# Output projections of a hybrid layer by seven block products instead of eight, with the gMLP phase's buffers kept to the end

## The chip, the cores and the metric

One core of a Trainium2 chip runs the whole layer as one program. The metric is the device time in microseconds, the median of several runs. Engines are called PE (matmul), PEld (its weight load), DVE (vector), ACT (scalar), POOL (GpSimd) and SP (which issues DMAs). Each engine works through its own row of instructions in order and waits where an operand is not there.

## The reference, cut to what matters

```python
proj = rms_norm(x, norm_g) @ w_in                    # 1024 x 1024 by 1024 x N_IN
u, v, z_a, z_b, xbc, dt_raw, g_a, g_b = split(proj)
v = layer_norm(gelu(v)); sv = einsum(tril(w_s), v) + b_s    # per chunk of 128 rows
y_a = gelu(u) * sv * silu(z_a)
y_b = gated_group_rms_norm(ssd_scan(...), z_b)       # 2048 columns
merged = sigmoid(g_a) * (y_a @ w_oa) + sigmoid(g_b) * (y_b @ w_ob)
x = x + merged @ w_out
x = x + sigmoid(rms_norm(x) @ w_pg) * (p @ w_ple)
out = rms_norm(x, final_g)
```

All is in 32-bit floats. The shapes are 1024 rows, width 1024; `w_oa` is 1024x1024, `w_ob` 2048x1024.

## The kernel before, in words

Every large product is made of three: each operand is split into a rounded part `hi` and a residue `lo`, and PE adds hi·hi, hi·lo and lo·hi, 128x512 at a time (L99 to L109). The split of a weight block (L229) is a cast on ACT (L231) and a subtraction on POOL (L232); the results lie in two tags of six buffers.

The phases follow each other: norm and transposes; the SSD branch in four groups; the gMLP phase; the output projections (o phase); `merged @ w_out` (`px`, stage 1); the gate of the last embedding (`ppg`) and the final norm.

The gMLP phase is 17 column pairs (L552): v0 to v3, ga3, then four times gb, za, u. A pair makes a 256 x 1024 piece of a projection, as a 2x2 by 2x2 block product by seven products of 12 matmuls where the plain way has eight. On the weights' side it needs four sums `s1` to `s4` (L561, DVE), seven casts and seven residues; on the side of the normed input the combinations `T1` to `T4` are made once (L527 to L547). Its results come out one by one through an epilogue: the first after the fourth product, the last, `epi(1, 0)`, after the seventh, `T4`. For v it is GELU, four transposes, batch statistics and a copy (L635); for za tanh and two updates on DVE (L682); for u GELU and a product (L691); for gb and ga one tanh (L608). In the program's text a pair's weights stand ahead of its matmuls.

The temporary tiles have tags of their own: epilogue `e` 5, sums `s` 4, `u5` 2, `sv` 4, `bt` 1.

The o phase (L710) has six parts: 512 rows of `y_b` with `w_ob` four times, of `y_a` with `w_oa` twice. A part reads y through POOL's DMA queue (L730), splits it (ACT, and DVE L734), and makes eight blocks `po` of 24 matmuls each; results are added into `m` (L758), in part 3 multiplied by the gate of g_b (L763), in parts 4 and 5 multiplied by that of g_a (L765) and added (L767, L769). After part 0 the pools of the gMLP phase are closed and larger ones opened.

The order on each engine is not the text's: a scheduler that simulates the program (L881) sets it, with the waits for free buffers that pools and tags bring.

Of the kernel before, what the change touches and what calls it, by code (L numbers as in the profile page):

```python
# [29 lines left out]
def kernel(  # L30
# [234 lines left out]
    dth = const.tile([P, NCH, NH], F32, name="dth")  # L265
    dec4 = const.tile([P, NCH, NH], F32, name="dec4")
    cdec = const.tile([P, NCH, NH], F32, name="cdec")
    cs = const.tile([P, NCH, NH], F32, name="cs")
# [280 lines left out]
    for j in range(2, 6):  # L549
        gate_tile(j)  # L550

    def pair(name, col, epi):  # L552

        blk = {}
        for i in range(2):
            raw = wp.tile([P, 4, 2 * P], F32, tag="raw", name=f"raw{i}_{name}")
            nc.sync.dma_start(out=raw, in_=w_in_k[:, 4 * i:4 * i + 4, col:col + 2 * P])
            blk[0, i], blk[1, i] = raw[:, :, 0:P], raw[:, :, P:2 * P]
        a11, a12, a21, a22 = blk[0, 0], blk[0, 1], blk[1, 0], blk[1, 1]
# [5 lines left out]
        A = {"B11": split_w(f"a11_{name}", a11)}  # L565
        s1 = sm("s1", a21, a22, ALU.add)
        A["T1"] = split_w(f"s1_{name}", s1)
        s2 = sm("s2", s1, a11, ALU.subtract)
        A["T2"] = split_w(f"s2_{name}", s2)
        A["B21"] = split_w(f"a12_{name}", a12)  # L570
        s3 = sm("s3", a11, a21, ALU.subtract)
        A["T3"] = split_w(f"s3_{name}", s3)
        s4 = sm("s4", a12, s2, ALU.subtract)
        A["B22"] = split_w(f"s4_{name}", s4)
        A["T4"] = split_w(f"a22_{name}", a22)
# [309 lines left out]
```

## Time and profile before

| | us |
|---|---|
| median of 3 runs | 1510.32 (1510.21 to 1511.16) |
| profiled execution: span | 1509.9 |
| profiled execution: time | 1511.94 |
| PE busy | 1464.8 (97%) |
| DVE busy | 825.2 (55%) |
| ACT busy | 680.6 (45%) |
| POOL busy | 657.3 (44%) |

The span runs from the first to the last instruction of the profiled execution; its time is 2.0 us more. A busy share is a mean over all phases. A matmul's record lasts longer than the distance to the next one, since they are pipelined; how many fit in a stretch is read from starts.

### The profile page before, as it was taken

To read this page: it belongs to the slowest core of one execution; us is meant where nothing else is said; L and a number is where in the kernel's file an instruction comes from. 1 tells how busy PE (TensorE), PEld (TensorE's weight loads), DVE (VectorE), ACT (ScalarE), POOL (GpSimd) and SP (SyncE) were. 2 spreads that over 40 slices of the span, in tenths; PEclk is the share of its full clock that TensorE was granted. 3 is DMA by queue.
4 is the path that set the end of the run, shared out by engine and by line. 5 is a ranking of instruction groups with operands and counts; after the bars stand their busy time and mean duration, and the time that the engine had idled before them with its cause. 6 is when DMAs were issued, how large, how long until landed. Compare 5 with 4: busy or idle time off the path is not lost.

```text
span 1509.9 us, 19002 instructions
## 1 busy us (share of the span) xinstructions
PE 1464.8 (97%) x7109; PEld 1206.0 (80%) x7109; DVE 825.2 (55%) x1194; ACT 680.6 (45%) x1220; POOL 657.3 (44%) x625
## 2 busy tenths in 40 slices
...
GB/s 271 112 74 56 84 70 56 127 70 85 46 136 71 70 112 92 35 139 56 125 113 133 97 114 84 91 126 132 143 129 93 131 186 181 194 118 144 221 175 65
DMA packets 130816, 172.02 MB, mean 114 GB/s; under 512 B 6964, under 2 KB 101380, under 8 KB 130724
## 3 DMA queue, kind: packets, MB, share of 16 engines
...
q10 hardware_dynamic: 228, 0.08, 0.0%
...
## 4 chain that ended last, share of the span: by engine, by line
PE 92%; DVE 2%; ACT 2%; DMA 1%; issue 1%; POOL 1%; SPq 0%; DVEq 0%; ACTq 0%; POOLq 0%
PE po L107 17%; PE ps_xs L107 12%; PE ps_zb L107 11%; PE px L107 6%; PE ppg L107 5%; PE ps_B L107 3%; PE ps_C L107 3%; PE x_za L581 3%; PE x_u L581 3%; PE x_gb L581 3%; PE x_v L581 3%; PE ps_ga L107 2%; PE pyd L407 2%; PE pyo L412 2%; PE pple L107 1%
## 5 line engine op out<-in xcount | busy, mean ns | idle before, releaser
L107 PE MATMUL po<-yh,hi_o 128*128 128x512 f32 x384 | 149.4, 389 | 0.0
L107 PE MATMUL po<-yl,hi_o 128*128 128x512 f32 x384 | 149.4, 389 | 0.0
L107 PE MATMUL po<-yh,lo_o 128*128 128x512 f32 x384 | 118.5, 389 | 0.0
L232 POOL TENSOR_TENSOR lo_o<-raw_o,hi_o 128x512 fp32r<-128x512 f32 x48 | 63.2, 1317 | 116.2 <-ACT hi_o L231 112.9
L107 PE MATMUL ps_zb<-hhi,hi_zb 128*128 128x512 f32 x256 | 101.5, 396 | 0.0
L107 PE MATMUL ps_zb<-hlo,hi_zb 128*128 128x512 f32 x256 | 101.3, 396 | 0.0
L107 PE MATMUL ps_xs<-hhi,hi_xs 128*128 128x512 f32 x256 | 100.7, 393 | 0.0
L107 PE MATMUL ps_xs<-hlo,hi_xs 128*128 128x512 f32 x256 | 100.1, 391 | 0.0
L231 ACT CAST hi_o<-raw_o 128x512 fp32r<-128x512 f32 x48 | 29.6, 621 | 137.5 <-PE po L107 109.4
L420 POOL TENSOR_TENSOR cv_xs<-cv_xs,ex 128x128 f32<-128x128 f32 x112 | 68.1, 633 | 40.7 <-DVE ex L415 40.6
L107 PEld LDWEIGHTS po<-yh,lo_o 128*128 128x128 f32 x384 | 72.1, 188 | 15.0
L107 PEld LDWEIGHTS po<-yh,hi_o 128*128 128x128 f32 x384 | 72.1, 188 | 15.0
L107 PEld LDWEIGHTS po<-yl,hi_o 128*128 128x128 f32 x384 | 72.1, 188 | 14.9
L400 ACT ACTIVATE lm<-lm,cs 128x128 f32<-128x128 f32 x256 | 78.6, 389 | 10.3 <-DMA lm<-csd 9.9
L107 PE MATMUL ps_zb<-hhi,lo_zb 128*128 128x512 f32 x256 | 81.5, 395 | 0.0
L232 POOL TENSOR_TENSOR lo_zb<-raw_zb,hi_zb 128x512 fp32r<-128x512 f32 x32 | 50.6, 1581 | 69.7 <-ACT hi_zb L231 69.7
L107 PE MATMUL ps_xs<-hhi,lo_xs 128*128 128x512 f32 x256 | 80.0, 391 | 0.0
L345 DVE SCALAR_TENSOR_TENSOR cv_xs<-ps_xs,cwT,cv_xs 128x1023 f32<-128x1023 f32 (+2 forms) x48 | 61.5, 1280 | 27.9 <-ACT cv_xs L342 26.9
L398 ACT ACTIVATE ex<-lm 64x512 f32<-64x512 f32 x56 | 35.2, 629 | 85.9 <-DMA lm<-csd 41.0
L232 POOL TENSOR_TENSOR lo_xs<-raw_xs,hi_xs 128x512 fp32r<-128x512 f32 x32 | 41.4, 1293 | 65.0 <-ACT hi_xs L231 65.0
L758 DVE TENSOR_TENSOR m<-m,po 128x512 f32<-128x512 f32 x48 | 30.8, 684 | 64.4 <-PE po L107 64.4
L734 DVE TENSOR_TENSOR yl<-yraw,yh 128x512 fp32r<-128x512 f32 x48 | 35.5, 775 | 44.5 <-ACT yh L733 43.1
...
## 6 DMA issues: line engine op xcount, KB each, us to landing
...
```

The costliest lines, as they stand in the source:

```text
L107: nc.tensor.matmul(o_, lhsT=a, rhs=b[h], start=(first and h not in seen), stop=(last and cnt[h] == 3))
L231: nc.scalar.copy(out=hi, in_=raw)
L232: (lo_on or nc.gpsimd.tensor_tensor)(out=lo, in0=raw, in1=hi.bitcast(F32), op=ALU.subtract)
L345: stt(out=a[:, sh:], in0=ps[:, :S - sh], scalar=cw(k, ci), in1=a[:, sh:], op0=ALU.mult, op1=ALU.add)
L398: act(ex[h * HD:(h + 1) * HD], lv[h * HD:(h + 1) * HD, :, h, :], AF.Exp)
L400: act(lm[:, r_, :], lm[:, r_, :], AF.Relu, bias=cs[:, c, g * HG + r_:g * HG + r_ + 1], scale=-1.0)
L407: nc.tensor.matmul(pyd[h * HD:(h + 1) * HD, (r_ // 2) * P:(r_ // 2 + 1) * P], lhsT=xdt[:, r_, :], rhs=lm[:, r_, :], start=True, stop=True)
L412: nc.tensor.matmul(pyo[:, j * P:(j + 1) * P], lhsT=hst[:, 2 * j:2 * j + 2, :].rearrange("s r d -> s (r d)"), rhs=cT[:, cl], start=True, st ...
L420: nc.gpsimd.tensor_tensor(out=xs[j][:, cl], in0=xs[j][:, cl], in1=ex[:, j, :], op=ALU.add)
L581: nc.tensor.matmul(pst, lhsT=l_[:, k, :], rhs=r_, start=(first and k == 0 and n_ == 0), stop=(k == 3 and n_ == 2), skip_group_check=True)
L734: tt(out=b[h], in0=raw[:, hsl[h]], in1=a[h].bitcast(F32), op=ALU.subtract)
L758: tt(out=mj, in0=mj, in1=pf, op=ALU.add)
```

## The change

The o phase uses the seven-product form too. `pair` (L552) is made general: it takes four blocks of weights, the number `nk` of 128-row blocks in each, the table of combinations on the other side, the epilogue and a tile for the sum `u5`; `in_pair` calls it for the gMLP phase with `nk` 4, the o phase with `nk` 2. A part of the o phase is four pairs of seven products of 6 matmuls. `part_b` makes the seven combinations of y for each part: four sums, seven casts, seven residues for each of two rows of blocks, shared out between DVE and POOL. y is read through SP's queue. The weights' residues of 128x256 are on POOL and so is the addition of the gated `y_a` products to `m`, which DVE did. The temporary tiles of the gMLP phase have one tag `g` of 16 tiles; the pool is kept, and `m`, the rows of x and later pieces use it and the tag `T`. A pair takes its four sum tiles at its start. Four small constants lie in one tile, which serves as `u5` in the o phase. Stage 1 takes its k rows in the order 4, 5, 0, 1, 2, 3, 6, 7, and loads x, x1 and pp by halves.

The diff, cut to its core:

```diff
@@ one tag for all temporary tiles of the gMLP phase, kept to the end @@
-    def g_tile(tag, name, bufs):
-        return g2.tile([P, 512], F32, tag=tag, name=name, bufs=bufs)
-    def e_tile(name):
-        return g_tile("e", name, 5)
+    def g_tile(name, dt=F32):
+        return g2.tile([P, 512], dt, tag="g", name=name, bufs=16)
...
-            t = g_tile("sv", f"sv{j}_{hf}", 4)
+            t = g_tile(f"sv{j}_{hf}")
...
@@ pair: for 4 or 2 rows of blocks @@
-    def pair(name, col, epi):
+    def pair(name, a11, a12, a21, a22, nk, B, epi, u5):
...
-        def sm(nm, a_, b_, op):
-            t = g_tile("s", f"{nm}_{name}", 4).rearrange("q (k c) -> q k c", c=P)
-            tt(out=t, in0=a_, in1=b_, op=op)
-            return t
+        def sums(n):
+            if nk == 2:
+                t = t4.tile([P, 4, nk, P], F32, tag="t4", name=f"s_{name}")
+                return [t[:, i_] for i_ in range(n)]
+            return [g_tile(f"s{i_}_{name}").rearrange("q (k c) -> q k c", c=P) for i_ in range(n)]
+        s1, s2, s3, s4 = sums(4)
+        A, both = {}, []
+        def split(c, raw):
+            if nk == 4:
+                A[c] = split_w(f"{c}_{name}", raw)
+                return
+            if not both:
+                both.append((w_part("wh", f"h{c}_{name}"), w_part("wl", f"l{c}_{name}")))
+                o_ = 0
+            else:
+                o_ = 2
+            hi, lo = [t_[:, o_:o_ + 2, :] for t_ in both[0]]
+            if o_:
+                both.pop()
+            nc.scalar.copy(out=hi, in_=raw)
+            ptt(out=lo, in0=raw, in1=hi.bitcast(F32), op=ALU.subtract)
+            A[c] = hi, lo
...
@@ o phase: y in seven combinations, a part ahead @@
-            nc.gpsimd.dma_start(out=raw, in_=src[row:row + P, :])
-            a, b = y_slots(pi, k, "h"), y_slots(pi, k, "l")
-            for h in range(2):
-                nc.scalar.copy(out=a[h], in_=raw[:, hsl[h]])
-                tt(out=b[h], in0=raw[:, hsl[h]], in1=a[h].bitcast(F32), op=ALU.subtract)
+    def part_b(pi):
...
+                nc.sync.dma_start(out=raw, in_=src[r0:r0 + P, :])
+                row += two(raw)
+            b11, b12, b21, b22 = row
+            def split(c, raw, lo_on):
+                hi, lo = Bp[c][k] = y_slots(pi, c, k)
+                nc.scalar.copy(out=hi, in_=raw)
+                lo_on(out=lo, in0=raw, in1=hi.bitcast(F32), op=ALU.subtract)
+            split("B11", b11, tt)
+            tt(out=b11, in0=b12, in1=b11, op=ALU.subtract)
+            split("T1", b11, ptt)
+            split("B22", b22, tt)
+            ptt(out=b12, in0=b22, in1=b12, op=ALU.subtract)
+            split("T3", b12, ptt)
+            tt(out=b22, in0=b22, in1=b11, op=ALU.subtract)
+            split("T2", b22, tt)
+            split("B21", b21, ptt)
+            tt(out=b21, in0=b21, in1=b22, op=ALU.subtract)
+            split("T4", b21, tt)
...
@@ o phase: matmuls and epilogue @@
-            ps = ps_two(f"po{pi}_{j}")
-            for k in range(4):
-                mm3(ps, wh[:, k, :], wl[:, k, :], yh[k], yl[k], k == 0, k == 3)
...
-                    tt(out=mj, in0=mj, in1=gh, op=ALU.add)
-                elif pi == 5:
-                    tt(out=gh, in0=mj, in1=gh, op=ALU.add)
-                    nc.scalar.copy(out=mhi[j][h], in_=gh)
...
+                stt(out=gh, in0=gh, scalar=1.0, in1=pf, op0=ALU.add, op1=ALU.mult)
+                ptt(out=mj, in0=mj, in1=gh, op=ALU.add)
+                if pi == 5:
...
+                    nc.scalar.copy(out=a, in_=mj)
+                    tt(out=b, in0=mj, in1=a.bitcast(F32), op=ALU.subtract)
+            pair(f"o{pi}_{mm}", raw[:, 0:2, 0:P], raw[:, 2:4, 0:P], raw[:, 0:2, P:2 * P], raw[:, 2:4, P:2 * P],
+                 2, Bp, epi, u5s[:, hsl[mm % 2]])
...
@@ stage 1: w_out and the tiles behind it @@
-    wo = [load_rows(f"wo{k}", w_out, k * P, *(w_slots if k in (4, 5) else big_slots)(f"wo{k}"))
-          for k in range(KD)]
+    korder = (4, 5, 0, 1, 2, 3, 6, 7)
+    wo = {k: load_rows(f"wo{k}", w_out, k * P, *(w_slots if k in (4, 5) else t_slots)(f"wo{k}")) for k in korder}
```

Where instructions move. ACT at the crossing from the pair za0 to u0, before (L231 is the cast of a weight block, `hi_s1` the cast for the product `T1`; L685 the activation on a result of za0):

```order
L596 COPY e_za0_7107<-x_za0_7065 128x512
L231 CAST hi_s2_u0_7191<-s2_u0_7189 128x512
L685 ACTIVATE zt000_7121<-a_za0_7078 128x512
L231 CAST hi_a12_u0_7195<-raw1_u0_7177 128x512
L685 ACTIVATE zt011_7138<-c_za0_7080 128x512
L231 CAST hi_s3_u0_7201<-s3_u0_7199 128x512
L231 CAST hi_s4_u0_7207<-s4_u0_7205 128x512
L589 COPY a_u0_7228<-x_u0_7215 128x512
L685 ACTIVATE zt001_7155<-e_za0_7107 128x512
L231 CAST hi_a22_u0_7211<-raw1_u0_7177 128x512
L685 ACTIVATE zt010_7171<-x_za0_7065 128x512
```

Now, where the cast for `T1` is `hi_T1` and the activation L704:

```order
L704 ACTIVATE zt000_7116<-a_za0_7074 128x512
L704 ACTIVATE zt011_7133<-c_za0_7076 128x512
L704 ACTIVATE zt001_7150<-e_za0_7102 128x512
L600 COPY a_u0_7224<-x_u0_7211 128x512
L704 ACTIVATE zt010_7166<-x_za0_7061 128x512
L231 CAST hi_T1_u0_7184<-s0_u0_7175 128x512
L231 CAST hi_T2_u0_7189<-s1_u0_7176 128x512
L231 CAST hi_B21_u0_7193<-raw1_u0_7172 128x512
L231 CAST hi_T3_u0_7198<-s2_u0_7177 128x512
L231 CAST hi_B22_u0_7203<-s3_u0_7178 128x512
```

Before, the casts of u0 alternate with the activations of za0; now the activation on the last result, `zt010`, stands ahead of the casts from `hi_T1` on.

PE at the same crossing, before (the moving operand, then the block of weights):

```order
L581 MATMUL x_za0_7065<-T4hB3_5636,hi_a22_za0_7061 128x512
L581 MATMUL x_za0_7065<-T4hA3_5635,lo_a22_za0_7062 128x512
L581 MATMUL c_u0_7230<-T100_5527,hi_s1_u0_7185 128x512
L581 MATMUL c_u0_7230<-T110_5528,hi_s1_u0_7185 128x512
L581 MATMUL c_u0_7230<-T100_5527,lo_s1_u0_7186 128x512
L581 MATMUL c_u0_7230<-T101_5559,hi_s1_u0_7185 128x512
L581 MATMUL c_u0_7230<-T111_5560,hi_s1_u0_7185 128x512
```

And now:

```order
L592 MATMUL x_za0_7061<-T4hB3_5633,hi_T4_za0_7057 128x512
L592 MATMUL x_za0_7061<-T4hA3_5632,lo_T4_za0_7058 128x512
L592 MATMUL c_u0_7226<-T100_5524,hi_T1_u0_7184 128x512
L592 MATMUL c_u0_7226<-T110_5525,hi_T1_u0_7184 128x512
L592 MATMUL x_u0_7211<-T200_5528,hi_T2_u0_7189 128x512
L592 MATMUL x_u0_7211<-T210_5529,hi_T2_u0_7189 128x512
L592 MATMUL c_u0_7226<-T100_5524,lo_T1_u0_7185 128x512
L592 MATMUL c_u0_7226<-T101_5556,hi_T1_u0_7184 128x512
L592 MATMUL c_u0_7226<-T111_5557,hi_T1_u0_7184 128x512
```

Behind the last product of za0 (`hi_a22`, now `hi_T4`) came twelve matmuls of `s1`; now two of `T1` and two of `T2`, which need casts alone, come ahead of the first that needs a residue.

POOL in part 4 of the o phase, before (L232 residue, L749 gate load, L730 y load):

```order
L749 DMA gt4_0_10142<-tad_608 128x1024
L232 TENSOR_TENSOR lo_o4_5_10261<-raw_o4_4_10254,hi_o4_5_10260 128x512
L730 DMA yraw5_1_10410<-yad_607 128x1024
L749 DMA gt4_1_10174<-tad_608 128x1024
L730 DMA yraw5_2_10418<-yad_607 128x1024
L232 TENSOR_TENSOR lo_o4_6_10331<-raw_o4_6_10328,hi_o4_6_10330 128x512
L749 DMA gt4_2_10216<-tad_608 128x1024
```

And now (L574 residue of 128x256, L806 the addition into `m`, L765 residue of y, L792 gate load):

```order
L574 TENSOR_TENSOR lT4_o4_1_10678<-raw_o4_1_10652,hT4_o4_1_10677 128x256
L574 TENSOR_TENSOR lB11_o4_2_10748<-raw_o4_2_10744,hB11_o4_2_10747 128x256
L574 TENSOR_TENSOR lT3_o4_1_10671<-s_o4_1_10654,hT3_o4_1_10670 128x256
L574 TENSOR_TENSOR lT2_o4_2_10756<-raw_o4_2_10744,hT2_o4_2_10755 128x256
L806 TENSOR_TENSOR m0_0_8940<-m0_0_8940,gt4_0_10620 128x512
L806 TENSOR_TENSOR m0_1_8958<-m0_1_8958,gt4_0_10620 128x512
L806 TENSOR_TENSOR m1_1_8949<-m1_1_8949,gt4_1_10631 128x512
L765 TENSOR_TENSOR yl5_T3_1_10983<-yraw5_1_0_10964,yh5_T3_1_10982 128x512
L806 TENSOR_TENSOR m1_0_8966<-m1_0_8966,gt4_1_10631 128x512
L792 DMA gt4_2_10712<-tad_605 128x1024
```

The additions into `m`, which were DVE's, stand on POOL between the residues of the pairs that come next.

## Rows read from the trace of the kernel before

**Rows 1.** The page: busy time, and the chain that ended last, by engine and line.

```profile
PE 1464.8 (97%) x7109; PEld 1206.0 (80%) x7109; DVE 825.2 (55%) x1194; ACT 680.6 (45%) x1220; POOL 657.3 (44%) x625
...
PE 92%; DVE 2%; ACT 2%; DMA 1%; issue 1%; POOL 1%; SPq 0%; DVEq 0%; ACTq 0%; POOLq 0%
...
PE po L107 17%; PE ps_xs L107 12%; PE ps_zb L107 11%; PE px L107 6%; PE ppg L107 5%; PE ps_B L107 3%; PE ps_C L107 3%; PE x_za L581 3%; PE x_u L581 3%; PE x_gb L581 3%; PE x_v L581 3%; PE ps_ga L107 2%; PE pyd L407 2%; PE pyo L412 2%; PE pple L107 1%
```

**Rows 2.** Busy time by stretches: us, engines (instructions), granted clock, DMA share, GB/s.

```profile
core 0: us, PE busy (x) PEld busy (x) DVE busy (x) ACT busy (x) POOL busy (x), PEclk, DMA share, GB/s
700.00:710.00 10.00, 3.84 (x7) 2.42 (x8) 7.77 (x7) 6.36 (x12) 8.72 (x6) 0.57 0.26 88
720.00:870.00 150.00, 147.42 (x704) 121.94 (x703) 80.87 (x178) 66.79 (x118) 63.09 (x49) 1.00 0.39 116
950.00:1060.00 110.00, 110.00 (x503) 91.56 (x503) 51.93 (x66) 46.73 (x83) 54.34 (x45) 1.00 0.37 119
```

**Rows 3.** The chain in order of time: start, length, what.

```profile
1040.83 2.72 PE x_za L581 x12
...
1059.87 258.63 PE po L107 x1141
```

**Rows 4.** ACT in order of time, third za pair into u: start, length, instruction.

```profile
977.63 0.62 ACT L231 CAST hi_s_u<-s_u 128x512 fp32r<-128x512 f32 x1 [1.21 <-PE e_za L581]
...
979.44 0.62 ACT L231 CAST hi_s_u<-s_u 128x512 fp32r<-128x512 f32 x1 [0.30 <-PE x_u L581]
...
982.57 0.62 ACT L231 CAST hi_a_u<-raw_u 128x512 fp32r<-128x512 f32 x1 [2.02 <-PE x_za L581]
...
983.09 0.59 ACT L685 ACTIVATE zt<-x_za 128x512 f32<-128x512 f32 x1
```

**Rows 5.** Groups of instructions of the gMLP pairs: count, busy, mean ns, idle before.

```profile
L231 ACT CAST hi_s_u<-s_u 128x512 fp32r<-128x512 f32 x16 | 9.9, 620 | 18.7 <-PE x_za L581 8.1 <-PE a_za L581 6.5 <-PE e_za L581 3.6
...
L685 ACT ACTIVATE zt<-x_za 128x512 f32<-128x512 f32 x4 | 2.4, 594 | 1.5 <-PE x_za L581 1.5
...
L232 POOL TENSOR_TENSOR lo_s_u<-s_u,hi_s_u 128x512 fp32r<-128x512 f32 x16 | 22.4, 1404 | 20.1 <-ACT hi_s_u L231 20.1
...
L644 DVE BATCH_NORM_STATS2 bst<-pv 128x6 f32<-128x128 f32 x64 | 14.2, 284 | 34.1 <-PE pv L642 34.1
```

**Rows 6.** PE in order of time in a v pair.

```profile
749.58 0.39 PE L581 MATMUL x_v<-hhi,lo_a_v 128*128 128x512 f32 x1
749.81 0.60 PE L642 MATMUL pv<-ident,vg 128*128 128x128 f32 x4
```

**Rows 7.** PE in order of time at the start of the gMLP phase.

```profile
706.16 2.07 PE L627 MATMUL pr<-lmA,onesr 128*128 128x512 f32 x2 [9.62 <-DVE lmA L624]
707.25 1.84 PE L581 MATMUL c_v<-T,hi_s_v 128*128 128x512 f32 x2
```

**Rows 8.** Groups of instructions on POOL and DVE: count, busy, mean ns, idle before.

```profile
L232 POOL TENSOR_TENSOR lo_o<-raw_o,hi_o 128x512 fp32r<-128x512 f32 x48 | 63.2, 1317 | 116.2 <-ACT hi_o L231 112.9 <-DMA yraw<-ybd 3.3
...
L420 POOL TENSOR_TENSOR cv_xs<-cv_xs,ex 128x128 f32<-128x128 f32 x112 | 68.1, 633 | 40.7 <-DVE ex L415 40.6
...
L749 POOL DMA_DIRECT2D gt<-tad x16 | 8.8, 548 | 34.7 <-DVE mlo L771 20.0 <-DVE m L767 14.1 <-DVE m L763 0.6
...
L563 DVE TENSOR_TENSOR s_gb<-raw_gb,raw_gb 128x512 f32<-128x512 f32 x4 | 2.8, 692 | 20.4 <-DMA raw_gb<-in_w_in_dram 20.4
...
L763 DVE SCALAR_TENSOR_TENSOR m<-gt,m 128x512 f32<-128x512 f32 x16 | 14.9, 961 | 0.0
```

**Rows 9.** POOL and DVE in order of time, both without pause.

```profile
667.37 1.75 POOL L539 TENSOR_TENSOR rT<-rB,rB 128x512 f32<-128x512 f32 x1
...
667.88 1.78 DVE L535 TENSOR_TENSOR rB<-hhi,hlo 128x512 f32<-128x512 f32 x1
...
669.08 1.74 POOL L539 TENSOR_TENSOR rT<-rB,rT 128x512 f32<-128x512 f32 x1
...
669.59 1.78 DVE L546 TENSOR_TENSOR T<-rT,T 128x512 fp32r<-128x512 f32 x1
```

More of the change, by code (lines that the diff above doesn't have):

```diff
@@ L263 @@
            scalar1=0.5, scalar2=None, op0=ALU.mult)
[L265 to L268, printed above, removed]
+    decs = const.tile([P, 4, NCH, NH], F32, name="decs")
+    dth, dec4, cdec, cs = [decs[:, i_] for i_ in range(4)]
     csd = dram.tile([NCH, NH, P], F32, name="csd")
@@ L549 @@
     for j in range(2, 6):
-        gate_tile(j)
-    def pair(name, col, epi):
[L554 to L559, printed above, removed]
-        def sm(nm, a_, b_, op):
-            t = g_tile("s", f"{nm}_{name}", 4).rearrange("q (k c) -> q k c", c=P)
-            tt(out=t, in0=a_, in1=b_, op=op)
-            return t
[L565 to L575, printed above, removed]
+        gatg_tile(j)
@@ L577, in prod @@
         def prod(pst, c, first):
-            for k in range(4):
+            for k in range(nk):
                 (ah, al), (bh_, bl_) = A[c], B[c][k]
@@ L592, in pair @@
         prod(xb, "T2", False)
-        u5 = g_tile("u5", f"u5_{name}", 2)
         nc.scalar.copy(out=u5, in_=cb)
@@ L668, in mix @@
         g, vj = j // 2, vjs.pop(j)
-        bt = g2.tile([P, P], F32, tag="bt", name=f"bt{j}", bufs=1)
+        bt = lmA[:, 4 + j % 4, :]
         stt(out=bt, in0=rsb[:, g, :], scalar=vec("lb", j), in1=bsb[:, g, :], op0=ALU.mult, op1=ALU.add)
@@ L710 @@
     parts = [(ybd, w_ob, i) for i in range(4)] + [(yad, w_oa, i) for i in range(2)]
-    m = [halves(F32, "hA", f"m{j}") for j in range(8)]
-    mhi, mlo = [], []
-    def y_slots(pi, k, i):
-        if pi == 0:
-            return [g2.tile([P, 512], F32R, tag="T", name=f"y{i}0_{k}_{h}", bufs=24) for h in range(2)]
-        if pi == 1:
-            return [hp_.tile([P, 512], F32R, tag="hB", name=f"y{i}1_{k}_{h}") for h in range(2)]
-        return two(big.tile([P, S], F32R, tag="big", name=f"y{i}{pi}_{k}"))
@@ new lines, with y_slots @@
+    m = [[None, None] for j in range(8)]
+    mhi, mlo = [None] * 8, [None] * 8
+    u5s = decs.rearrange("q a c h -> q (a c h)")
+    def y_slots(pi, c, k):
+        n = 4 * COMBOS.index(c) + 2 * k
+        r = []
+        for i, nm in ((n, "h"), (n + 1, "l")):
+            if pi % 2:
+                tg = "hA" if i < 4 else "T"
+            else:
+                tg = "hA" if i % 7 in (0, 2, 4) else "hB"
+            name = f"y{nm}{pi}_{c}_{k}"
+            r.append(g2.tile([P, 512], F32R, tag=tg, name=name, bufs=24) if tg == "T" else
+                     hp_.tile([P, 512], F32R, tag=tg, name=name))
+        return r
@@ new lines, in part_b @@
+    def part_b(pi):
+        src, w, kp = parts[pi]
+        Bp = {c: [None, None] for c in COMBOS}
+        blk = []
+        for k in range(2):
+            row = []
+            for i in range(2):
+                r0 = (kp * 4 + 2 * i + k) * P
+                raw = t4.tile([P, S], F32, tag="lm", name=f"yraw{pi}_{k}_{i}", bufs=2)
+                nc.sync.dma_start(out=raw, in_=src[r0:r0 + P, :])
[16 more added lines that the diff above has]
+            split("T4", b21, tt)
+        return Bp
```

180 lines of the change are left out of this document (100 added, 80 removed).

## The prediction

> **What bounds the kernel now.** I read the page's busy shares and chain of waits first. TensorE (PE) is busy for 97% of the span and carries 92% of the chain; the output projections (`po`) alone are 17% [rows 1]. So the end is set by PE, and what counts is where PE works without a gap. The table by stretches answers that: in the gMLP pairs PE is busy 110.00 of 110 us, and in the v pairs, the only place there with holes, it idles 2.6 of 150 us [rows 2]. The chain in order of time then gives the pace: twelve 128x512 matmuls in 2.72 us, and one unbroken piece of 1141 `po` matmuls in 258.63 us, 0.2267 us each [rows 3]. Every matmul taken out is therefore worth 0.2267 us, and every wait put in front of PE is paid in full: there is no slack into which it could fall.
>
> **What goes.** The o phase has 6 parts of 4 column pairs with 48 matmuls a pair, 1152 in all. With seven block products of 6 matmuls a pair has 42, in all 1008. 144 x 0.2267 = 32.6 us less. The additions that buy this are priced below.
>
> **What moves in the gMLP phase.** The five temporary pools become one, and four sum tiles are taken at the start of a pair. No matmul there changes, but the order does. Before, ACT's casts of the next pair's weights stand between the activations of the present pair. The trace shows this at the third za-to-u crossing: casts `hi_s_u` at 977.63 and 979.44, `hi_a_u` at 982.57, and only then the last activation `zt` at 983.09 [rows 4]. Changed, all six casts of the next pair from `hi_T1` on stand behind that last activation, at each of the 16 crossings between the 17 pairs. That activation reads the last product of the present pair, and PE has nothing after this product but work that needs the six casts. So PE must wait for a round trip that did not exist before.
>
> Its price by rows: a matmul lasts 0.39 us though the next starts after 0.23 [rows 6], ACT's activation takes 0.594 us, the cast 0.620 us [rows 5]. That is 1.60 from the start of the last matmul to the first one of `T1`, of which 0.23 is the last one's own slot: PE stands for at least 1.4 us. PE then finds two matmuls that need only `hi_T1` and two of `hi_T2` (0.9 us), and waits for `lo_T1` on POOL, 1.32 to 1.75 us after the cast (the `lo_s_u` mean is 1.404) [rows 5, 8, 9]. `hi_T2` needs a sum that DVE now does behind the last `zt` update.
> - za to u (4) and u to gb (3): 1.4, plus the lag of POOL behind the 0.9 us of work, plus DVE's late sum: 2.0 to 3.5, I take 2.7. 7 x 2.7 = 18.9.
> - gb to za (4): transposed mixing products stand on PE between and cover part: 1.3. 5.2. ga to gb (1): 1.6.
> - v to v (3) and v to ga (1): the last activation is followed by four transposes on PE (0.60 us [rows 6]), four batch statistics of 0.284 us on DVE and a copy on ACT [rows 5], and only behind them come the first sum and cast. 0.4 + 0.6 + 0.6 + 1.1 + 0.7 + 0.6 = 4.0, then the lag for `lo_T1`: 4 to 6. I take 5 and, with the table load before ga, 6: 21.
>
> Sum 46.7; I take 45. The low end is 16 x 1.4 = 22 and the high end 60. What is late next behind these waits is nothing: ACT, DVE and POOL are idle about half of the time there, so the lost time is not given back by them later.
>
> **What is added in the o phase.** A pair now lasts 42 x 0.2267 = 9.5 us on PE, a part 38.1. Per part POOL gets 28 residues `lo` of 128x256, 8 y operations of 128x512, in parts 3 to 5 also 8 DMA issues, and in parts 4 and 5 the 16 gate adds, which stand in its row ahead of weights that PE is about to need. The trace has no 128x256 on POOL. Lower bound: half of `lo_o`, 1.317/2 = 0.66; upper: between the 128x128 mean of 0.633 and 1.317 on a line, 0.86 [rows 8]. I take 0.70, near the half, because the 128x128 operations stand in a crowded stretch. That gives POOL 28 x 0.70 + 8 x 1.317 = 30.1 in parts 0 to 3, and 30.1 + 21.1 + 8 x 0.548 = 55.6 in part 4; in part 5, which prepares no next y, 19.6 + 21.1 + 4.4 = 45.1. Both exceed 38.1 before anything disturbs them.
>
> And something does. Where both engines work from SBUF without pause, a POOL operation takes 1.74 and the next one starts 1.71 later, with one DVE operation fitted into each [rows 9]. Against POOL's 1.317 alone one such DVE operation costs POOL 0.39, a 256-wide one, by halves, 0.2. DVE has per part 14 such y operations and 16 weight sums (8.8), 16 `m` products more in part 3 and 16 `mlo` in part 5 (6.4). Load on the pair of them: parts 0 to 2 38.9, part 3 45.3 to 49.7 (with the DMA issues), part 4 60.0 to 64.4, part 5 50.3 to 54.7. Over 38.1 that is 2.4 + 7.2..11.6 + 21.9..26.3 + 12.2..16.6, 44 to 57 in all. From it go the lead that 12 buffered weight combinations give (12 x 1.36 = 16) and about 8 us of the next product (`px`) that need not the last two rows of `m`: 20 to 33. I take 24. With 0.66 and no disturbance, parts 4 and 5 exceed by 16 and 6, and lead and drain cover it: 0. With 0.86 it is some 27 more: 60.
>
> By the page "SBUF — State Buffer", section "SBUF: two separate sides" (the Trainium skill), the port pair that DVE and GpSimd share is an exclusive lock for a whole instruction and the loser blocks fully. By that rule a DVE operation would cost its whole 0.692 [rows 8] instead of 0.39, and the o phase would lose about 45 us more; [rows 9] speak for part of it only, since 1.71 is less than 1.317 + 0.692.
>
> **Small things.** At the start of gMLP the mask product `lmA`, for which PE waits 9.62 us today [rows 7], stands behind two more DVE sums, but fewer pool waits stand before it: -2 to +3, taken +1. y comes through SP's queue instead of POOL's, a part ahead; it is hidden behind 38 us of products unless SP's queue is held by a weight load that waits for a buffer. Stage 1 and the last product issue more, shorter DMAs off the path: 0 to 5, taken 0. ACT in the o phase has per pair 7 casts of 256 columns, 3.5 of 512 for y and 3 copies; even at 0.620 [rows 5] for each that is 8.4 of 9.5 us. DVE in part 3 has 14 y operations and 24 additions on PSUM at 0.692, 16 `m` products at 0.961 [rows 8] and 16 sums of half that size: some 47 us against 38.1. That is the excess of part 3 seen from the other engine and is not added again.
>
> **Sum.** The profiled run took 1511.9 (span 1509.9 and 2.0 around it), 1.6 over the median of 1510.3. 1511.9 - 32.6 + 45 + 24 + 1 = 1549.3; on the median's footing 1547.7, rounded to 1547.
>
> **Rivals.**
> - *The saving outweighs (faster).* Place: the crossings and part 4. If each crossing costs only the bare round trip (22 us) and POOL's overload is all taken by lead and drain (0), the time is 1510.3 - 32.6 + 22 + 1 = 1501. It turns where both losses together fall under 32. For it: ACT and POOL are idle half the time, and buffers for 12 combinations are there. Against it: the v crossings alone make 16 of it. If nothing were lost at all it would be 1478; the order on ACT excludes that.
> - *Losses about equal the saving.* Bare crossings (22) and 10 in parts 4 and 5: 1511.
> - *The port locks fully* (the rule above, as a mechanism of this kernel: DVE's 14 y operations and 16 sums stop POOL for their whole time). 45 more: 1592. For it: operations on DVE stretch from 0.692 to 1.78 [rows 8, 9]; against it: the pair's pace of 1.71.
> - *The clock falls at each crossing.* After the one gap of 9.62 us the granted clock was 0.57 in the next stretch, its lower level for most of it, and two `c_v` matmuls took 1.84 instead of 0.45 [rows 2, 7]. If each of 16 gaps did this for some 2 us: 32 more, 1579. Against it: these gaps are a quarter to a half as long. The v crossings may do it (+8, inside the range).
>
> **How the numbers follow.** What this kernel's measurement can tell from no change is about 0.2%, 3 us. Likeliest case, both losses as worked out: 0.62, 1520 to 1572, time 1547. Faster rival 0.12, of which 0.11 lies under 1507. Equal 0.06, half of it within 3 us. Full lock 0.08, clock 0.12. So faster 0.11, within 0.04, slower 0.85. The range leaves out most of the faster rival and the upper half of the two slow ones: 1506 to 1580.
>
> **What would show it.** In the changed profile PE should have a hole in front of the first `T1` matmul (`c_u`, `c_gb`, `c_za`, `c_v`) of nearly each pair, put down to ACT's `hi_T1` or POOL's `lo_T1`, longest in the v pairs; the gMLP stretch should be 22 to 60 us longer; the o phase should have no waits in parts 0 to 2 and waits on POOL's `lo` in parts 4 and 5. I am wrong if PE stays at full share over the crossings, if the o phase comes out at 229 us, or if its waits name DMAs on SP or ACT's casts instead.

## The result: slower, and the profile after

The changed kernel takes 1650.54 us (median of 4, 1649.62 to 1650.91) against 1510.74 of the kernel before (4 runs, 1510.21 to 1513.41). The ratio is 1.0921, its 95% interval 1.0902 to 1.0939: 140 us slower. I had forecast 1547 and at most 1580: the right sign, and about a quarter of the size.

The page of the profile after, the same three lines as [rows 1]:

```profile
PE 1496.8 (91%) x6965; PEld 1203.0 (73%) x6965; DVE 964.6 (59%) x1350; ACT 770.5 (47%) x1464; POOL 860.7 (52%) x829
...
PE 27%; DVE 9%; issue 4%; POOL 3%; ACT 2%; DMA 2%; DVEq 0%; ACTq 0%; POOLq 0%
...
PE ppg L107 5%; PE px L107 5%; PE x_o L592 3%; PE x_u L592 2%; PE x_za L592 2%; PE x_gb L592 2%; POOL lT_o L574 1%; PE c_u L592 1%; DVE yl_B L765 1%; PE c_gb L592 1%; PE c_o L592 1%; DMA raw_o<-in_w_ob_dram 1%; PE c_za L592 1%; PE a_o L592 1%; DVE s_o L582 1%
```

PE does 6965 instructions instead of 7109, 144 fewer as counted, and its share falls from 97% to 91%, of a longer span. The chain is no longer PE's: 27% instead of 92%, and it runs through all engines.

Busy time by stretches after: two v pairs to ga, gMLP pairs, parts 0 to 2 of the output projections, part 4 (columns as in [rows 2]):

```profile
core 0: us, PE busy (x) PEld busy (x) DVE busy (x) ACT busy (x) POOL busy (x), PEclk, DMA share, GB/s
720.00:840.00 120.00, 91.21 (x371) 71.25 (x370) 43.53 (x111) 40.56 (x71) 36.27 (x27) 0.80 0.27 79
960.00:1080.00 120.00, 107.74 (x454) 86.08 (x453) 52.24 (x73) 40.82 (x73) 48.92 (x38) 0.94 0.23 72
1152.00:1290.00 138.00, 120.03 (x484) 93.61 (x485) 111.90 (x140) 80.97 (x180) 111.61 (x109) 0.95 0.33 108
1345.00:1400.00 55.00, 41.96 (x152) 32.48 (x151) 32.54 (x44) 17.58 (x40) 46.22 (x52) 0.81 0.36 125
```

Where PE had almost no hole (2.6 of 150 us in the v pairs, none in the others [rows 2, 3]) it now has 29 of 120 us in the v pairs, 12 of 120 in the gMLP pairs and 18 of 138 in the first parts, and the granted clock, 1.00 in those stretches before, is 0.80, 0.94 and 0.95. From the starts of the matmuls I made an account. A matmul of 512 columns is given a slot of 0.2267 us, a transpose or one of 128 columns 0.077, the same before and after. Time in which PE stands before a matmul beyond that slot is "waiting"; where matmuls follow each other later than their slots without standing, it is "slow".

| | before | after | difference |
|---|---|---|---|
| gMLP: first `T1` product of v0 to first `o` matmul, us | 347.2 | 427.1 | +79.9 |
| of it waiting, slow | 3.2, 11.0 | 59.5, 39.9 | +56.3, +28.9 |
| o phase: from there to the first `px` matmul | 263.8 | 319.0 | +55.2 |
| of it waiting, slow | 0, 0 | 61.2, 25.2 | +61.2, +25.2 |
| from there to the end | 191.6 | 197.8 | +6.2 |

With 2.3 us gained ahead of gMLP that is the 139 us by which the span grew. (Some matmuls of a phase stand behind the first of the next one, so the rows do not sum to slots exactly; 18 of the o phase, 4.1 us, lie in the last row after. In the o phase, 32.6 us of matmuls less and 86.4 of waiting and slow ones give +53.8.)

The waits of PE after (engine, line, releaser: total us, times, longest):

```profile
engine line waited for: us in total, times, longest us
...
PE pv L661 <- ACT vg L658: 16.8, 8, 2.1
...
PE x_o L592 <- DVE c_o L610: 11.9, 7, 3.6
...
PE c_o L592 <- ACT a_o L600: 10.8, 3, 7.2
...
PE x_o L592 <- ACT e_o L606: 9.1, 6, 3.1
...
PE c_v L592 <- ACT hi_T_v L231: 6.8, 3, 2.3
...
PE c_u L592 <- ACT hi_T_u L231: 6.3, 4, 2.7
...
PE x_o L592 <- POOL lT_o L574: 0.5, 1, 0.5
```

In [rows 2, 3] there was nothing of the kind. The first, `pv`, and the two on `hi_T` are the crossings; the three on `c_o`, `a_o` and `e_o` are the o phase, and they name neither a residue on POOL nor a DMA, but the copies and additions with which a pair is finished. POOL's residues of the weights are named for 0.5 us in all.

A crossing from v0 to v1 in order of time, all engines:

```profile
729.77 1.05 PE L661 MATMUL pv<-ident,vg 128*128 128x128 f32 x4 [2.10 <-ACT vg L658]
...
730.85 0.89 DVE L663 BATCH_NORM_STATS2 bst<-pv 128x6 f32<-128x128 f32 x4 [2.25 <-PE pv L661]
...
731.78 0.59 ACT L665 COPY vt<-pv 128x512 f32<-128x512 f32 x1 [2.06 <-DVE bst L663]
...
732.26 0.60 ACT L658 ACTIVATE vg<-x_v 128x512 f32<-128x512 f32 x1
...
732.91 1.12 PE L661 MATMUL pv<-ident,vg 128*128 128x128 f32 x4 [2.10 <-ACT vg L658]
...
736.31 1.22 PE L592 MATMUL c_v<-T,hi_T_v 128*128 128x512 f32 x2 [2.28 <-ACT hi_T_v L231]
...
738.18 0.63 PE L592 MATMUL a_v<-hhi,hi_B_v 128*128 128x512 f32 x1
...
738.61 0.63 PE L592 MATMUL a_v<-hlo,hi_B_v 128*128 128x512 f32 x1
```

Behind the last product come three groups of transposes, not one. Two of them wait 2.10 us each for a GELU, which on ACT stands behind the copy `vt` of the group before, which waits for the statistics of that group (730.85, 731.78, 732.26). So the round trip of 3.1 us is run through twice before the one to the casts, and `c_v` starts at 736.31. And once it starts, matmuls follow 0.43 us apart (738.18, 738.61) instead of 0.2267. The granted clock of this stretch, and of the one at the crossing from za0 to u0 that is shown next:

```profile
729.50:740.50 11.00, 6.35 (x19) 4.59 (x20) 5.36 (x12) 5.31 (x10) 4.16 (x3) 0.53 0.54 158
...
904.00:910.50 6.50, 5.25 (x12) 4.13 (x13) 3.38 (x4) 2.92 (x6) 5.23 (x4) 0.50 0.30 81
```

It is near 0.5, the lower of two levels, in both; ahead of the first PE had stood once for 2.10 us, ahead of the second for 1.19 us and, after two matmuls, was standing again.

The crossing from za0 to u0:

```profile
901.49 0.60 ACT L704 ACTIVATE zt<-x_za 128x512 f32<-128x512 f32 x1 [1.87 <-PE x_za L592]
...
901.98 0.61 ACT L231 CAST hi_T_u<-s_u 128x512 fp32r<-128x512 f32 x1
...
902.64 0.73 PE L592 MATMUL c_u<-T,hi_T_u 128*128 128x512 f32 x2 [1.19 <-ACT hi_T_u L231]
...
902.66 1.27 POOL L232 TENSOR_TENSOR lo_T_u<-s_u,hi_T_u 128x512 fp32r<-128x512 f32 x1 [11.77 <-ACT hi_T_u L231]
...
902.72 1.76 DVE L579 TENSOR_TENSOR s_u<-s_u,raw_u 128x512 f32<-128x512 f32 x1
...
904.57 0.62 ACT L231 CAST hi_T_u<-s_u 128x512 fp32r<-128x512 f32 x1 [1.99 <-DVE s_u L579]
...
905.25 1.22 PE L592 MATMUL x_u<-T,hi_T_u 128*128 128x512 f32 x2 [1.87 <-ACT hi_T_u L231]
```

The last activation, then the cast, then PE, exactly as forecast; PE stands 1.19 us. The next stop is longer: the sum for `T2` starts on DVE 0.06 us after POOL has begun a residue, and takes 1.76 us instead of 0.69; POOL's took 1.27. DVE was done 0.55 us after POOL, and the cast and PE's two `T2` matmuls (905.25, 1.87 us of standing) wait for it.

In the o phase, end of part 1:

```profile
1243.83 1.15 DVE L765 TENSOR_TENSOR yl_T<-yraw,yh_T 128x512 fp32r<-128x512 f32 x1
...
1244.38 1.18 POOL L574 TENSOR_TENSOR lT_o<-raw_o,hT_o 128x256 fp32r<-128x256 f32 x1
...
1244.90 0.69 DVE L610 TENSOR_TENSOR c_o<-x_o,decs 128x512 f32<-128x512 f32 x1
...
1245.64 0.50 PE L592 MATMUL x_o<-yh_T,hT_o 128*128 128x512 f32 x1 [1.80 <-DVE c_o L610]
...
1246.77 0.75 POOL L574 TENSOR_TENSOR lB_o<-raw_o,hB_o 128x256 fp32r<-128x256 f32 x1
```

PE stands 1.80 us for `c_o`, an addition of 0.69 us on DVE that frees a bank. It stands in DVE's row behind `yl_T` (1.15 us). That operation and POOL's residue lie on each other: the latter takes 1.18 instead of 0.75 (1246.77).

The longest wait of the phase, in part 4:

```profile
1369.77 4.46 DVE L584 TENSOR_TENSOR s_o<-raw_o,s_o 128x256 f32<-128x256 f32 x1
1369.82 0.74 POOL L574 TENSOR_TENSOR lB_o<-s_o,hB_o 128x256 fp32r<-128x256 f32 x1
...
1373.24 0.71 POOL L574 TENSOR_TENSOR lT_o<-raw_o,hT_o 128x256 fp32r<-128x256 f32 x1
...
1376.18 0.77 PE L592 MATMUL c_o<-yh_T,hB_o 128*128 128x512 f32 x1 [7.20 <-ACT a_o L600]
```

One sum of 128x256 on DVE, which takes 0.41 us where it is undisturbed, takes 4.46 us here. It ends 0.28 us after a run of six residues that POOL makes without pause from 1369.82 to 1373.95. What finishes the pair stands behind it in DVE's row, and PE stands for 7.20 us.

Busy time in parts 1 and 2, from the first matmul of each to that of the next:

```profile
1194.90:1245.60 50.70, 42.57 (x168) 33.27 (x168) 44.56 (x59) 28.54 (x64) 42.81 (x42) 0.93 0.31 101
1245.60:1290.60 45.00, 39.97 (x169) 31.21 (x170) 37.33 (x48) 23.86 (x54) 36.91 (x38) 1.00 0.36 121
```

DVE is busy for 44.6 and 37.3 us, POOL for 42.8 and 36.9, where PE's matmuls take 38.1.

The groups of the o phase on POOL and DVE after (count, busy, mean ns, idle before):

```profile
L574 POOL TENSOR_TENSOR lT_o<-s_o,hT_o 128x256 fp32r<-128x256 f32 x69 | 63.1, 927 | 7.9 <-ACT hT_o L573 7.8
...
L806 POOL TENSOR_TENSOR m<-m,gt 128x512 f32<-128x512 f32 x27 | 38.0, 1422 | 1.8 <-DVE gt L805 1.7
...
L765 DVE TENSOR_TENSOR yl_B<-yraw,yh_B 128x512 fp32r<-128x512 f32 x22 | 26.3, 1194 | 4.0 <-ACT yh_B L764 4.0
...
L584 DVE TENSOR_TENSOR s_o<-raw_o,s_o 128x256 f32<-128x256 f32 x21 | 18.8, 897 | 0.3
...
L610 DVE TENSOR_TENSOR c_o<-x_o,decs 128x512 f32<-128x512 f32 x23 | 15.9, 692 | 22.4 <-issue 12.8 <-PE x_o L592 9.4 <-ACT decs L604 0.2
```

A 128x256 residue, for which I took 0.70 between 0.66 and 0.86, costs 0.91 on the mean of all its groups (0.93 in the one shown), the gate addition 1.42 instead of 1.317, and a y residue on DVE 1.02 to 1.19 instead of the 0.692 of an operation of that size in [rows 8]. Only DVE's additions from PSUM are unmoved at 0.69.

### The profile page after: what moved, and what is told of

The parts are those of the page before. It is cut to its first block, busy times and chain, and to the rows that moved or that the text cites. A ratio compares the mean times of both kernels' runs of the same rounds, so it can differ in the third digit from the quotient of the medians.

```text
span 1648.8 us, 19454 instructions
## 1 busy us (share of the span) xinstructions
PE 1496.8 (91%) x6965; PEld 1203.0 (73%) x6965; DVE 964.6 (59%) x1350; ACT 770.5 (47%) x1464; POOL 860.7 (52%) x829
## 5 line engine op out<-in xcount | busy, mean ns | idle before, releaser
L592 PE MATMUL x_o<-yh_T,hT_o 128*128 128x512 f32 x144 | 62.9, 437 | 30.4 <-DVE c_o L610 11.9
L232 POOL TENSOR_TENSOR lo_zb<-raw_zb,hi_zb 128x512 fp32r<-128x512 f32 x32 | 49.7, 1554 | 69.7 <-ACT hi_zb L231 69.7
L399 ACT ACTIVATE lm<-lm,decs 128x128 f32<-128x128 f32 x256 | 78.9, 392 | 10.2 <-DMA lm<-csd 9.8
L232 POOL TENSOR_TENSOR lo_xs<-raw_xs,hi_xs 128x512 fp32r<-128x512 f32 x32 | 41.4, 1293 | 65.2 <-ACT hi_xs L231 65.2
L574 POOL TENSOR_TENSOR lT_o<-s_o,hT_o 128x256 fp32r<-128x256 f32 x72 | 66.0, 930 | 7.9 <-ACT hT_o L573 7.8
L592 PEld LDWEIGHTS x_o<-yh_T,hT_o 128*128 128x128 f32 x144 | 28.9, 201 | 46.5 <-DVE c_o L610 15.7
L592 PE MATMUL x_o<-yh_T,lT_o 128*128 128x512 f32 x144 | 59.9, 416 | 0.5 <-POOL lT_o L574 0.5
L592 PE MATMUL x_o<-yl_T,hT_o 128*128 128x512 f32 x144 | 59.9, 416 | 0.0
L107 PEld LDWEIGHTS ps_xs<-hhi,lo_xs 128*128 128x128 f32 x256 | 48.1, 188 | 10.1
L107 PEld LDWEIGHTS ps_xs<-hhi,hi_xs 128*128 128x128 f32 x256 | 48.1, 188 | 9.9
L107 PEld LDWEIGHTS ps_xs<-hlo,hi_xs 128*128 128x128 f32 x256 | 48.1, 188 | 9.8
L107 PEld LDWEIGHTS ps_zb<-hlo,hi_zb 128*128 128x128 f32 x256 | 48.1, 188 | 9.5
L107 PEld LDWEIGHTS ps_zb<-hhi,lo_zb 128*128 128x128 f32 x256 | 47.6, 188 | 10.1
```

Source lines behind the costliest of these rows:

```text
L107: nc.tensor.matmul(o_, lhsT=a, rhs=b[h], start=(first and h not in seen), stop=(last and cnt[h] == 3))
L232: (lo_on or nc.gpsimd.tensor_tensor)(out=lo, in0=raw, in1=hi.bitcast(F32), op=ALU.subtract)
L399: act(lm[:, r_, :], lm[:, r_, :], AF.Relu, bias=cs[:, c, g * HG + r_:g * HG + r_ + 1], scale=-1.0)
L574: ptt(out=lo, in0=raw, in1=hi.bitcast(F32), op=ALU.subtract)
L592: nc.tensor.matmul(pst, lhsT=l_[:, k, :], rhs=r_, start=(first and k == 0 and n_ == 0), stop=(k == nk - 1 and n_ == 2), skip_group_check=True)
```

## The experiments

"Own tags" stands below for the changed kernel with separate tags (second run). The kernel before took 1512 to 1513 us beside these runs.

**One tag in the kernel before.**

```diff
-        return g2.tile([P, 512], F32, tag=tag, name=name, bufs=bufs)
+        return g2.tile([P, 512], F32, tag="g", name=name, bufs=16)
...
-    bst = g2.tile([P, NCH, 8, 6], F32, name="bst")
+    bst = t4.tile([P, NCH, 8, 6], F32, tag="t4", name="bst")
...
-        bt = g2.tile([P, P], F32, tag="bt", name=f"bt{j}", bufs=1)
+        bt = lmA[:, 4 + j % 4, :]
```

> The kernel before with one edit: all temporary tiles of the gMLP phase share one tag of 16 (as in the changed kernel; two small tiles are moved out of the pool to make room). The output projections stay with eight products. Theory A (the shared tag alone moves the casts of the next pair behind the last activation of the present one): the gMLP phase is longer by what the changed kernel's is, about 88 us (some 59 us of waits and 29 us of matmuls at a lower clock), so 1590 to 1605 us. Rival B (the sums taken at the start of a pair, or the general form of the pair, are the cause): 1505 to 1520 us.

Measured: 1596.57 us, ratio 1.0555 (1.0532 to 1.0578). By the account gMLP takes 434.4 us with 58.9 of waiting and 39.7 slow, the o phase is as before (261.9). Busy time in the v pairs:

```profile
720.00:840.00 120.00, 91.22 (x378) 71.31 (x377) 37.89 (x99) 40.26 (x70) 33.62 (x25) 0.82 0.27 81
```

The same 91.2 of 120 us as the changed kernel. Theory A holds: the tag alone does it, without the new form of `pair`.

**Own tags in the changed kernel.**

```diff
-    def g_tile(name, dt=F32):
-        return g2.tile([P, 512], dt, tag="g", name=name, bufs=16)
+    TAGS = {"e": 5, "s": 4, "u5": 2, "sv": 4, "w": 1}
+    turn = [t_ for t_, n_ in TAGS.items() for _ in range(n_)]
+    taken = [0]
+    def g_tile(name, dt=F32, tag=None):
+        if tag is None:
+            tag = turn[taken[0] % 16]
+            taken[0] += 1
+        return g2.tile([P, 512], dt, tag=tag, name=name, bufs=TAGS[tag])
...
-            return [g_tile(f"s{i_}_{name}").rearrange("q (k c) -> q k c", c=P) for i_ in range(n)]
+            return [g_tile(f"s{i_}_{name}", tag="s").rearrange("q (k c) -> q k c", c=P) for i_ in range(n)]
```

> The changed kernel with tags of their own for the gMLP phase's temporary tiles again (5, 4, 2, 4 and 1, the same 16 tiles); all else, the seven products of the output projections among it, as changed. Theory A: the gMLP phase is as short as before (347 us from the first T1 product to the output projections), the output projections stay at about 307 us for 229 us of matmuls: 1555 to 1570 us. Rival B: it stays over 1630 us.

Measured: 1568.22 us, ratio 1.0373 (1.0347 to 1.0400). gMLP 346.3 us with 3.2 of waiting, the o phase 307.9. On ACT the casts of u0 alternate with the activations of za0 again. So the sums that are taken at the start of a pair are not to blame, and the two losses are separate: 84 us with the tag alone and 55 with the o phase alone, 139 in all, against 140 with both.

**Which sharing it is.** In the kernel before, sums and epilogue tiles in one tag of 9, with the two small tiles `bst` and `bt` moved as in the first run, the rest as it was:

```diff
+        tag, bufs = ("es", 9) if tag in ("e", "s") else (tag, bufs)
         return g2.tile([P, 512], F32, tag=tag, name=name, bufs=bufs)
```

> The kernel before, where only the tags of the pair's sums (4) and of the epilogue tiles (5) become one of 9; u5 and sv keep theirs. If that sharing is the part of the single tag that moves the casts, the gMLP phase loses what the run with one tag lost: 1588 to 1605 us. If the number of tiles that share, or the other two tags, matter too, it is between: 1520 to 1580 us.

Measured: 1588.6 us, ratio 1.0508 (1.0477 to 1.0538); gMLP 423.1. And all but the sums in one tag of 11, the two small tiles moved here too:

```diff
+        tag, bufs = ("eu", 11) if tag in ("e", "u5", "sv") else (tag, bufs)
         return g2.tile([P, 512], F32, tag=tag, name=name, bufs=bufs)
```

> The kernel before, where epilogue tiles, u5 and sv share one tag of 11 and the sums keep theirs. If only sums sharing with epilogue tiles matters: 1508 to 1516 us. If any sharing does: over 1530 us.

Measured: 1510.16 us, ratio 0.9985 (0.9972 to 0.9999). The v pairs of the first and of the second:

```profile
720.00:840.00 120.00, 91.23 (x371) 70.81 (x370) 43.53 (x110) 39.98 (x70) 35.73 (x26) 0.82 0.27 79
```

```profile
720.00:840.00 120.00, 119.65 (x577) 99.12 (x576) 58.62 (x142) 58.30 (x101) 53.15 (x42) 1.00 0.41 123
```

So what costs 76 us (one tag of 9) to 84 us (one of 16) is that a pair's sums share a tag with the epilogue tiles of the pair ahead of it; sharing among the others, and moving the two small tiles, costs nothing. Why the scheduler holds the sums back there is not settled.

**y made once.**

```diff
-        Bp = part_b(pi)
+        if pi == 0:
+            Bp = part_b(pi)
```

> As the run with own tags, but the seven combinations of y are made for the first part alone and used for all six parts (left out: the y operands of parts 1 to 5, their loads, casts, sums and residues). Theory L (POOL and DVE stop each other; their sum of work is the bound): 14 DVE and 8 POOL operations of 128x512 a part go, some 19 us of the two engines' common time in each of 5 parts; the output projections fall from 307 to 245 to 260 us, the time to about 1500 to 1515 us. Theory Q (POOL's row alone, 10 us less of 30 to 56 a part): 25 to 35 us less than own tags. Theory C (the chain copy, add, next bank is too long for products of 6 matmuls): within 10 us of own tags.

Measured: 1521.27 us, ratio 1.0062 (1.0039 to 1.0085), 47 less than own tags; the o phase is 257.0. Between L and Q by the total, but parts 1 to 3 run at 38.1 us each without one wait. What is left is 10.9 us in part 0, 19 in parts 4 and 5, where the gate additions are, and one wait of 7.5 us in front of a `px` matmul. C is wrong: the same chains of copies and additions hold up nothing here.

**No residues.**

```diff
-                both.append((w_part("wh", f"h{c}_{name}"), w_part("wl", f"l{c}_{name}")))
+                both.append((w_part("wh", f"h{c}_{name}"),) * 2)
...
-            ptt(out=lo, in0=raw, in1=hi.bitcast(F32), op=ALU.subtract)
-            A[c] = hi, lo
+            A[c] = hi, hi
```

> As the run with own tags, but in the output projections the residues of the weights are not made; the rounded part stands in their place (left out: 168 POOL subtractions of 128x256; the matmuls are as many). Theory L: about 20 us a part less on POOL and no more blocking of DVE by it; output projections 235 to 255 us, time 1490 to 1510 us. Theory Q: the same or a little more, since POOL's row is then nearly empty: 1490 to 1500 us. Theory C: within 10 us of own tags.

Measured: 1517.87 us, ratio 1.0041 (1.0023 to 1.0058), 50 less than own tags, a little short of both L and Q. Taking either of two loads away, that on POOL or the one mostly on DVE, gives some 50 us: both rows are nearly full together. Part 1 of this run:

```profile
1104.20:1146.40 42.20, 39.02 (x170) 31.27 (x170) 35.14 (x56) 26.09 (x60) 15.75 (x12) 1.00 0.39 122
```

DVE's operations are the same as with own tags, and it is busy for 35.1 us of 56 instructions, there 42.5 of 55 (below). Its y residues take 0.74 and 0.93 us where they took 1.03 and 1.22, two of its four sums 0.53 where they took 0.70 and 0.76; the other two stay, and one y sum rises from 1.17 to 1.35. So POOL's residues do lengthen DVE's operations on the whole.

**Both left out.**

> As the run with own tags, with both left out: y combinations after part 0, and the weights' residues of the output projections. Theory L: nothing is left to overload either engine; parts 1 to 5 at their matmul time of 38.1 us, only the start of the phase and the gates in part 5 cost: 1490 to 1503 us. Theory C (the chain copy, add, next bank of short products is too long by itself): waits on a_o, c_o and e_o stay in parts 1 to 4, over 1515 us.

Measured: 1496.69 us, ratio 0.9900 (0.9865 to 0.9934): parts 1 to 4 at their matmul time, 6.6 us lost at the start, 3.1 in part 5, and 7.6 behind it. The o phase takes 239.6 us, 24 less than before. Only with both left out is the kernel faster than before, and then by 15.5 us, half of the 32.6.

**Gate additions on DVE again.**

```diff
-                ptt(out=mj, in0=mj, in1=gh, op=ALU.add)
+                tt(out=mj, in0=mj, in1=gh, op=ALU.add)
```

> As the run with own tags (1568 us), but the 16 additions of the gated y_a products to m in each of parts 4 and 5 are on DVE again. Theory Q (POOL's row is what is late): 21 us a part less on POOL, 20 to 30 us faster, 1538 to 1548 us. Theory L (each of the two engines holds up the other, DVE's row is full as well): the addition costs DVE 0.69 to 1.1 us, parts 4 and 5 gain 5 to 12 us together at most: 1553 to 1565 us.

Measured: 1538.46 us, ratio 1.0176 (1.0139 to 1.0213), 30 less. Here Q was right and L wrong: in parts 4 and 5 POOL's row is late, and the addition, 0.82 us on DVE for 1.42 on POOL, costs less there. Part 5 loses 3.5 us instead of 14.6, part 4 10.6 instead of 17.7.

**y on DVE too.**

```diff
@@ part_b: six residues and two sums, from POOL to DVE @@
-            split("T1", b11, ptt)
+            split("T1", b11, tt)
...
-            ptt(out=b12, in0=b22, in1=b12, op=ALU.subtract)
+            tt(out=b12, in0=b22, in1=b12, op=ALU.subtract)
...
```

> As the run with own tags and the gate additions on DVE (1538 us), and the 8 y operations a part that POOL had (six residues, two sums) are on DVE too, so POOL keeps the weights' residues alone. Theory Q (POOL's row is late in parts 1 to 4): about 10 us a part less on POOL, 20 to 40 us faster, 1500 to 1518 us. Theory L (both engines' work counts together, where one stops the other): POOL gives back 1.3 and DVE takes 0.6 per operation, 5 us a part, 1512 to 1528 us. Theory D (DVE's row is the full one): DVE gets 5 to 8 us a part more, 1560 to 1575 us.

Measured: 1528.72 us, ratio 1.0112 (1.0095 to 1.0129), 10 less than with the gates alone, just past L's range. Part 1 by engines, with own tags, with y made once (part 1 too), and here:

```profile
1112.00:1159.00 47.00, 39.37 (x159) 30.11 (x159) 42.52 (x55) 25.90 (x60) 42.34 (x41) 0.96 0.30 101
```

```profile
1110.00:1148.00 38.00, 38.00 (x170) 31.37 (x168) 23.41 (x39) 17.14 (x44) 22.33 (x30) 1.00 0.17 56
```

```profile
1110.00:1155.00 45.00, 42.81 (x176) 33.72 (x176) 42.65 (x66) 27.66 (x62) 25.77 (x29) 0.96 0.38 118
```

With own tags DVE is busy 42.5 and POOL 42.3 of 47 us; with y made once 23 and 22 of 38, and PE 38.00; here DVE is busy 42.7 of 45 and POOL 26. Now DVE alone is full. Moving work from one to the other shifts the bound and doesn't remove it.

**Zeros for residues.**

```diff
-            ptt(out=lo, in0=raw, in1=hi.bitcast(F32), op=ALU.subtract)
+            nc.gpsimd.memset(lo.bitcast(F32), 0.0)
```

> As the run with own tags, but POOL writes zeros into the residue tiles of the output projections instead of subtracting (left out: the residues; the 168 instructions stay on POOL, as writes that read nothing and wait for no cast). If POOL's reading from the on-chip memory is what stops DVE, DVE's sums and y residues come down from 0.9 to 1.2 us to near 0.7 and the time falls to that of the run without residues, 1515 to 1525 us, even where POOL stays busy. If any operation of POOL stops DVE for its whole time, or POOL's row is the bound, it falls only by what the writes are shorter.

Measured: 1515.76 us, ratio 1.0024 (1.0011 to 1.0037). The write on POOL and a sum on DVE in this run, and the sum with own tags:

```profile
L581 POOL MEMSET lT_o<- 128x256 f32 x120 | 34.4, 315 | 33.7 <-PE x_o L599 18.9 <-PE c_o L599 6.8 <-PE a_o L599 6.1
...
L591 DVE TENSOR_TENSOR s_o<-raw_o,s_o 128x256 f32<-128x256 f32 x24 | 11.8, 491 | 0.4
```

```profile
L591 DVE TENSOR_TENSOR s_o<-raw_o,s_o 128x256 f32<-128x256 f32 x24 | 15.1, 628 | 0.3
```

A write takes 0.315 us, a third of a residue, so POOL is emptier by 100 us as well and the run doesn't tell the two readings apart by its total. The sum on DVE comes down from 0.628 to 0.491, two others from 0.755 to 0.557 and from 0.695 to 0.598, while the fourth rises from 0.592 to 0.758. DVE's y residues take 0.78 and 0.95 us, about as much as without residues (0.74 and 0.93), though POOL still has its 168 instructions; that speaks for POOL's reads, not its writes, as what stops DVE, but does not show it, since the writes are also shorter.

**Sums in a tag of their own, gates on DVE, in the changed kernel.**

```diff
-    TAGS = {"e": 5, "s": 4, "u5": 2, "sv": 4, "w": 1}
+    TAGS = {"r": 12, "s": 4}
...
-                ptt(out=mj, in0=mj, in1=gh, op=ALU.add)
+                tt(out=mj, in0=mj, in1=gh, op=ALU.add)
```

> The changed kernel with two tags instead of one for the gMLP phase's temporary tiles: the pair's sums have 4 of their own, all others share 12; gate additions on DVE. If only the sharing of sums with epilogue tiles moves the casts, the gMLP phase is as with own tags: 1535 to 1545 us. If sharing among the others costs too: 1550 to 1600 us.

Measured: 1540.08 us, ratio 1.0184 (1.0163 to 1.0204): as with five tags and the same gates (1538.5). Two tags instead of one mend the gMLP phase. The best version with the seven products and nothing left out is 1528.7, still 1% above the kernel before; none beats it.

## Why the prediction was wrong, point by point

- *144 matmuls less, 32.6 us*: right. The count is right and the pace holds where nothing waits (38.1 us a part with y made once).
- *The casts behind the last activation at each crossing*: right in place and sign, and shown by the runs with one tag and own tags. In size it was 79.9 us instead of 45, for the two reasons that follow.
- *The v crossings, 5 us each*: the step that failed first. I counted one round trip through transposes, statistics and copy. There are three in a row, two of 3.1 us for the transposes (16.8 us in 8 waits) and one to the cast. By the account, from the middle of one pair to the middle of the next, v to v loses 10.4 us each, 7.4 of it waiting, instead of 5, and v to ga 16.0 instead of 6. za to u loses 5.2 to 6.2 and u to gb 5.3 instead of 2.7; of each 3.4 is waiting, inside the 2.0 to 3.5 that I gave, made up of the cast behind the last activation and of the late sum on DVE that lies beside POOL's residue; the rest is slow. ga to gb and most of gb to za came near their price (2.1 for 1.6; 1.3 to 1.9, once 4.6, for 1.3).
- *The clock falls at each crossing*: put down as a rival with 0.12. It came true in part: +28.9 us in gMLP, the granted clock 0.80 over the v pairs and 0.94 over the others. I had held against it that these gaps are a quarter to a half as long as the one of 9.62 [rows 7]; a gap of 2.10 us, and gaps of 1.19 and 1.87 us with two matmuls between, stand where the granted clock fell to 0.53 and 0.50, with matmuls 0.43 us apart. So the two matmuls of 1.84 us in [rows 7], which I put down to the clock, hold more than its price: two at that pace take 0.86. The page "TensorE: Matmul & The Clock Gate" of the Trainium skill, "HAM oscillation — how this bites in real kernels", describes such a kernel, whose waits throttle PE again and again. The v pairs agree in that: 0.53 over 729.5 to 740.5, and again over 760 to 771. The runs never separate this from the waits: no run keeps the one without the other.
- *POOL's row in parts 4 and 5*: right. With the gate additions moved off it, 30 us come back, 18 of them in these two parts by the account.
- *The o phase loses 24 us*: 86 by the account, the largest error; by parts 16.6, 12.7, 6.8, 11.5, 23.4 and 15.4. Parts 3 to 5 came as I had priced them before anything was taken off (7.2 to 11.6 and 34 to 43). What failed is parts 0 to 2, 2.4 us in my sum and 36 in the run, and the next point. The step that failed is the sum over both engines. POOL's row in parts 1 and 2 was right on the mean (42.8 and 36.9 us for 38.9). DVE's I did not add up there, and I did not charge it for what POOL's operations cost it: a y operation takes 0.9 to 1.2 us, a sum of 256 columns 0.6 to 0.9. By the means over the o phase DVE's row is 14 x 1.06 + 16 x 0.73 + 24 x 0.69 = 43 us a part, by the undisturbed times 32; it was busy for 44.6 and 37.3. So a second row is as long as the 38.1 of matmuls and must also wait for them. I had worked out DVE's row for part 3 only: some 47 us, and 47.5 in the run. The signs that I named fail here too: waits stand in parts 0 to 2, and they name copies and additions and once, for 5.4 us, a cast of y, not POOL's `lo`.
- *24 us taken off for lead and drain*: not found. Weights that are ready ahead do not help when the addition that frees a bank is what is late.
- *The rule of the page "SBUF — State Buffer"* (the Trainium skill, "SBUF: two separate sides"), that the loser blocks for the whole instruction: I set it aside because of the pace of 1.71 us in [rows 9]. The row of 902.72 comes near it: 1.76 us beside 1.27, DVE done 0.55 after POOL. The row of 1369.77 goes further, a DVE operation that ends only behind six of POOL's. My rival with 0.08 priced this as 45 us on POOL's row, which came out as in the main case; the loss fell on DVE's row. Its 1592 is nearer to the result than 1547, but by luck. The rival of the clock came about on top of the main case, and I had treated it as an alternative.
